# Batched 64x64 matmul: the left operand transposed into its block diagonal by VectorE, and loaded in 8 KB runs

## The chip, the cores and the metric

The kernel runs on one core of one Trainium2 chip. The metric is the time of one execution on the device in microseconds (us), as the median of several runs; a profile of one execution gives the span from its first to its last instruction.

## The reference

Inputs are `a` and `b`, both 1024 x 64 x 64 in fp32, and the output is their product matrix by matrix, in fp32:

```python
def reference(a, b):
    return np.matmul(a, b).astype(np.float32)
```

Each array is 16.78 MB. The kernel multiplies in bf16 and sums in fp32.

## The kernel before, in words

The 1024 products are done in 16 tiles of 64 (`t`). Four matrices are multiplied at a time. TensorE sums over the 128 partitions, so the kernel gives each of four matrices 32 partitions: a partition holds one pair of neighbouring k. The pair is two bf16 values, and the kernel treats it as one 4-byte word wherever it only moves data (`bitcast(fp32)`). The weights of a matmul are a block diagonal `at_bd`: on the 32 partitions of matrix h only the columns of matrix h are filled, with its transposed a, and the rest stays zero from a memset at the start. There are two such buffers (`N_BD`), used in turn. For each group of four matrices `multiply` (L189) issues two halves of the columns (`j`) times the two members of the pair (`u`), 64 matmuls of 128x64 a tile.

How a gets into `at_bd`:

- `load_a` (L73, L77) fetches 128 matrices (an `s`, two tiles) in runs of 4 KB, 128 partitions a DMA. Three quarters of them are cast to bf16 by the load on GpSimd's queue, with `single_packet`; the last quarter comes plain, in fp32, on SP's queue. The first 128 matrices come plain on both SP's and ScalarE's queue (`load_first_a`, L90).
- `regroup` (L105, L108, L111) copies, and where needed casts, them into `a_bf`, on VectorE.
- `transpose` (L120) turns 128x128 words at a time on TensorE, with an identity, into PSUM, 16 for each `s`; ScalarE copies the result to `at_sb` (L123), and reorders it.
- `spread` (L133) copies from `at_sb` into the four diagonal blocks, four VectorE copies of 32x1024 words a tile.

b is loaded a tile at a time (L96, on SP's queue for even `t` and on ScalarE's for odd), three tiles ahead (`B_AHEAD`), and cast to bf16 by VectorE (L144; the first on ScalarE, the last in quarters on both). The products lie in PSUM and are copied to `o_sb` in pieces of 64x512 (L177), mostly by ScalarE, with 14 of them by VectorE. A tile is stored one tile later (`HOLD`), from GpSimd's queue, and the last two tiles from SP's and ScalarE's (L166).

The order on each engine is the order of the calls, written out by hand (`manual_schedule`). In the loop over `t` come `spread(t+1)`, `cast(t+1)`, the load of b three tiles ahead, a load of a, a transpose for the next `s`, `multiply(t)`, and then `regroup`, another transpose and the store of the tile before. An instruction waits at the head of its engine's queue for its inputs and for its buffer; everything behind it on that queue waits with it. `a_pool` holds three `s`, `o_pool` eight tiles.

Of the kernel before, what the change touches and what calls it, by code (L numbers as in the profile page):

```python
# [7 lines left out]

fp32 = mybir.dt.float32
# [4 lines left out]
def kernel(  # L14
# [7 lines left out]

    nc = tc.nc
    B, M, K = a.shape  # L30
    _, _, N = b.shape
    assert (M, K, N) == (64, 64, 64) and B % 128 == 0

    n_t, n_s = B // 64, B // 128
    A_AHEAD = 3
    B_AHEAD = 3
    N_BD = 2
    HOLD = 2

    a_v = a.rearrange("(s g h) (mp v) k -> s h g mp (v k)", h=4, g=32, v=16)  # L40
    b_v = b.rearrange("(t g h) (kp u) n -> t (h kp) g (u n)", h=4, g=16, u=2)
    o_v = out.rearrange("(t gh x) (mo w) n -> t (x mo) gh (w n)", gh=8, x=8, w=4)

    consts = ctx.enter_context(tc.tile_pool(name="consts", bufs=1))
    a_pool = ctx.enter_context(tc.tile_pool(name="a_pool", bufs=A_AHEAD))
    b_pool = ctx.enter_context(tc.tile_pool(name="b_pool", bufs=B_AHEAD))
    work = ctx.enter_context(tc.tile_pool(name="work", bufs=2))
    o_pool = ctx.enter_context(tc.tile_pool(name="o_pool", bufs=8))
    t_psum = ctx.enter_context(
        tc.tile_pool(name="t_psum", bufs=4, space=bass.MemoryType.PSUM)  # L50
    )
    o_psum = ctx.enter_context(
        tc.tile_pool(name="o_psum", bufs=2, space=bass.MemoryType.PSUM)
    )

    bd_tiles = [
        consts.tile([128, 2, 16, 2, 4, 16], fp32, name=f"at_bd{i}") for i in range(N_BD)
    ]
    identity = consts.tile([128, 128], fp32)
    warm = consts.tile([128, 2], fp32)  # L60
    a_tiles, b_tiles, abf_tiles, at_tiles, bbf_tiles = {}, {}, {}, {}, {}
    held = {}

    def store_queue(t, lo):
        if t < n_t - 2:
            return nc.gpsimd
        return nc.scalar if t == n_t - 1 and lo % 4 == 0 else nc.sync

    def load_a(s):

        a_sb = a_pool.tile([128, 3, 16, 64], bf16, name="a_sb")
        for h in range(3):
            nc.gpsimd.dma_start(  # L73
                out=a_sb[:, h, :, :].rearrange("p v k -> p (v k)"), in_=a_v[s, h], single_packet=True
            )
        a_raw = a_pool.tile([128, 16, 64], fp32, name="a_raw")
        nc.sync.dma_start(out=a_raw[:].rearrange("p v k -> p (v k)"), in_=a_v[s, 3])  # L77
        a_tiles[s] = a_sb, a_raw

    def load_first_a():  # L80

        raw = [
            o_pool.tile([128, 8, 2, 2, 64], fp32, name="o_sb")[:].rearrange(
                "p gh j wl n -> p (gh j wl n)"
            )
            for _ in range(2)
        ]
        parts = [raw[h % 2][:, 1024 * (h // 2) : 1024 * (h // 2) + 1024] for h in range(4)]
        for h in range(4):
            (nc.scalar if h % 2 else nc.sync).dma_start(out=parts[h], in_=a_v[0, h])  # L90
        a_tiles[0] = parts

    def load_b(t):
        b_sb = b_pool.tile([128, 16, 128], fp32, name="b_sb")
# [1 line left out]
        queue.dma_start(out=b_sb[:], in_=b_v[t])  # L96
        b_tiles[t] = b_sb

    def regroup(s):
        a_sb = a_tiles.pop(s)  # L100
        a_bf = work.tile([128, 16, 4, 64], bf16, name="a_bf")
        if s == 0:
            for h in range(4):
                copy = nc.scalar.copy if h % 2 else nc.vector.tensor_copy
                copy(a_bf[:, :, h, :], a_sb[h].rearrange("p (v k) -> p v k", v=16))  # L105
        else:
            cast_sb, raw = a_sb
            nc.vector.tensor_copy(  # L108
                a_bf[:, :, 0:3, :], cast_sb[:].rearrange("p h v k -> p v h k")
            )  # L110
            nc.vector.tensor_copy(a_bf[:, :, 3, :], raw[:])  # L111
        abf_tiles[s] = a_bf
        at_tiles[s] = work.tile([128, 2, 32, 2, 4, 4], fp32, name="at_sb")

    def transpose(s, j):
        a_cols = abf_tiles[s][:].rearrange("p v h k -> p v (h k)").bitcast(fp32)
        for wl in range(2):
            at_ps = t_psum.tile([128, 4, 128], fp32, name="at_ps")
            for vo in range(4):
                nc.tensor.transpose(  # L120
                    at_ps[:, vo, :], a_cols[:, 4 * vo + 2 * j + wl, :], identity[:]
                )
            nc.scalar.copy(  # L123
                at_tiles[s][:, j, :, wl, :, :],
                at_ps[:].rearrange("p vo (g mp) -> p g mp vo", mp=4),
            )

    def spread(t):
        half = slice(16 * (t % 2), 16 * (t % 2) + 16)
        bd = bd_tiles[t % N_BD]  # L130
        for h in range(4):
            rows = slice(32 * h, 32 * h + 32)
            nc.vector.tensor_copy(  # L133
                bd[rows, :, :, :, h, :].rearrange("p j g wl mo -> p j (g wl) mo"),
                at_tiles[t // 2][rows, :, half, :, :, :].rearrange(
                    "p j g wl mp vo -> p j (g wl) (mp vo)"
                ),
            )

    def cast(t):  # L140
# [15 lines left out]
            piece()  # L156

    def multiply(t):
        at_bd = bd_tiles[t % N_BD][:].rearrange("p j g wl h mo -> p j g (wl h mo)")
        at_bd = at_bd.bitcast(bf16).rearrange("p j g (c u) -> p j g c u", u=2)  # L160
        b_bf = bbf_tiles.pop(t)
        last = t == n_t - 1
# [6 lines left out]
            )  # L169

        def evacuate(o_ps, gh, n, copies):

            for par in range(2):
                for wl in range(2):
                    src = o_ps[64 * wl : 64 * wl + 64, :, par, :, :]
                    dst = o_sb[64 * par : 64 * par + 64, gh : gh + n, :, wl, :]
                    copies[2 * par + wl](dst, src)  # L177

        for half in range(2):
            if not last:  # L180
                o_ps = o_psum.tile([128, 4, 2, 2, 64], fp32, name="o_ps")
            for g8 in range(8):
                if last and g8 % 4 == 0:
                    o_ps = t_psum.tile([128, 2, 2, 2, 64], fp32, name="at_ps")
                g = 8 * half + g8
                gl = (g8 % 4 if last else g8) // 2
                for j in range(2):
                    for u in range(2):
                        nc.tensor.matmul(  # L189
                            o_ps[:, gl, g % 2, j, :],  # L190
                            at_bd[:, j, g, :, u],
                            b_bf[:, g, 64 * u : 64 * u + 64],
                            start=(u == 0),
                            stop=(u == 1),
                        )
                if last and g8 % 4 == 3:
                    copy = nc.scalar.copy if g8 == 3 else nc.vector.tensor_copy
                    evacuate(o_ps, g // 4 * 2, 2, [copy] * 4)
            if not last:
                copies = [nc.scalar.copy] * 4  # L200
                if half and t % 2:
                    copies[2:] = [nc.vector.tensor_copy] * 2
                evacuate(o_ps, 4 * half, 4, copies)
        if last:
            held[t] = [lambda q=q: put(2 * q, 2) for q in range(4)]
        else:
# [1 line left out]
            held[t] = [lambda q=q: put(q, 8 if whole else 4) for q in ([0] if whole else [0, 4])]  # L208

    with tc.manual_schedule():  # L210
        load_first_a()

        nc.vector.memset(warm[:, 0:1], 0.0)
        nc.scalar.copy(warm[:, 1:2], warm[:, 0:1])  # L214
        load_b(0)
        load_b(1)
        nc.vector.memset(bd_tiles[0][:], 0.0)  # L217
        make_identity(nc, identity)
        nc.gpsimd.memset(bd_tiles[1][:, 0], 0.0)
        load_a(1)  # L220
        load_b(2)
        nc.gpsimd.memset(bd_tiles[1][:, 1], 0.0)
        load_a(2)
        regroup(0)
        transpose(0, 0)
        transpose(0, 1)
        spread(0)
        cast(0)
        for t in range(n_t):
            s, half = t // 2, t % 2  # L230
            if t + 1 < n_t:
                spread(t + 1)
                cast(t + 1)
            if t + B_AHEAD < n_t:
                load_b(t + B_AHEAD)
            if half == 0 and 0 < s < n_s - 1 - A_AHEAD:
                load_a(s + 1 + A_AHEAD)
            if half == 0 and 0 < s < n_s - 1:
                transpose(s + 1, 1)
            multiply(t)  # L240
            if t == 0:
                regroup(1)
                load_a(A_AHEAD)
                load_a(A_AHEAD + 1)
                transpose(1, 0)
                transpose(1, 1)
            elif t == 1:
                regroup(2)
            elif half == 0 and s + 2 < n_s:
                regroup(s + 2)  # L250
            if half == 1 and s + 2 < n_s:
                transpose(s + 2, 0)
            if t >= HOLD - 1:
                store(t - HOLD + 1)
        for t in range(n_t - HOLD + 1, n_t):
            store(t)
# [30 lines left out]
```

## Time and profile before

| What | Value |
| --- | --- |
| median of 3 runs | 134.8 us (134.71 to 134.83) |
| span of the profiled execution | 133.4 us |
| busy: TensorE matmul / weight load | 64.4 / 61.1 us |
| busy: VectorE | 94.6 us (71%), 120 instructions |
| busy: ScalarE | 87.9 us (66%), 161 instructions |
| busy: GpSimd | 33.0 us (25%) |
| packets of the DMA engines | 45.01 MB, mean 337 GB/s |
| mean granted TensorE clock | 0.785 of full speed |

The span lies 1.4 us under the median; it leaves out what is before the first and after the last instruction. A group of the profile names the line and engine, the operation, what is written and read with their shapes (partitions x elements), how often it ran, then busy time in us and the mean of one in ns, and after the bar how long the engine stood idle just before and who ended most of that. In the slices of the span each digit is the busy share of one fortieth, in tenths. Packets of loads that cast are counted by the bytes they write, half of what they read.

### The profile page before, as it was taken

The numbers are of one execution on the slowest core, as the hardware profiler recorded it, in microseconds if no ns is written. First come the engines' busy times: TensorE is split into PE (matmuls) and PEld (weight loads), VectorE is DVE, ScalarE is ACT, GpSimd is POOL, SyncE is SP. The second block draws the span as 40 slices with busy tenths as digits, with TensorE's granted clock in tenths as the row PEclk, the third lists the DMA queues.
The fourth block names the chain that finished last, engine by engine and source line by source line (L and its number), as shares of the span: only waits on it lengthen the run. The fifth ranks groups of instructions, "written<-read, shape, count | busy, mean of one in ns | idle before, by whom it ended". The sixth has DMA issues, their size and how long they took to land.

```text
span 133.4 us, 2837 instructions
## 1 busy us (share of the span) xinstructions
PE 64.4 (48%) x1152; PEld 61.1 (46%) x1152; DVE 94.6 (71%) x120; ACT 87.9 (66%) x161; POOL 33.0 (25%) x43
## 2 busy tenths in 40 slices
PE   0006406960089384289518970956197363970000
PEld 0006306950089274189418950945196363960000
DVE  5930399109998809995999699959999995987000
ACT  3225424999036998969595969696968969099600
POOL 8991000420090070341233021203020410300000
PEclk9999975797557999856985699599959955599555
DMA  3999999999999999999999999999999999999990
GB/s 77 371 329 311 307 311 281 284 306 325 327 312 401 316 320 333 399 384 397 311 281 375 406 389 351 304 316 390 394 396 387 396 392 391 402 405 398 382 319 18
DMA packets 19021, 45.01 MB, mean 337 GB/s; under 512 B 1088, under 2 KB 3136, under 8 KB 19008
## 3 DMA queue, kind: packets, MB, share of 16 engines
q0 software_dynamic: 6832, 20.19, 50.1%
q1 hardware_dynamic: 7120, 14.68, 30.4%
q10 hardware_dynamic: 5056, 9.96, 19.7%
q8 instruction: 9, 0.15, 0.4%
q14 instruction: 4, 0.03, 0.1%
HBM read 33.55 MB, written 16.78 MB: 377 GB/s over the span
## 4 chain that ended last, share of the span: by engine, by line
DMA 53%; DVE 15%; ACT 13%; PE 6%; issue 5%; SPq 2%; DVEq 0%; ACTq 0%
DMA b_sb<-in_b_dram 53%; ACT o_sb L177 9%; DVE at_bd L133 6%; PE o_ps L189 4%; DVE b_bf L144 4%; DVE o_sb L177 3%; PE at_ps L120 2%; ACT at_sb L123 2%; ACT b_bf L144 1%; SPq L90 1%; DVE a_bf L108 1%; SPq L96 1%; ACT b_bf L151 1%; DVE a_bf L111 0%; SPq L77 0%
## 5 line engine op out<-in xcount | busy, mean ns | idle before, releaser
L177 ACT COPY o_sb<-o_ps 64x512 f32<-64x512 f32 x106 | 61.5, 580 | 10.3 <-PE o_ps L189 9.0
L189 PEld LDWEIGHTS <-at_bd 128*128 128x128 bf16 x1024 | 42.3, 113 | 39.5 <-DVE b_bf L144 25.7
L189 PE MATMUL o_ps<-b_bf,at_bd 128*128 128x64 bf16 x960 | 42.6, 216 | 35.4 <-DVE b_bf L144 23.4
L133 DVE COPY at_bd<-at_sb 32x1024 f32<-32x1024 f32 x64 | 46.9, 733 | 14.1 <-ACT at_sb L123 11.8
L120 PE MATMUL at_ps<-identity,a_bf 128*128 128x128 f32 x128 | 21.2, 335 | 19.4 <-ACT a_bf L105 11.2
L166 POOL DMA_DIRECT2D out_dram<-o_sb x14 | 15.4, 1097 | 56.9 <-ACT at_sb L123 23.4
L120 PEld LDWEIGHTS at_ps<-identity,a_bf 128*128 128x128 f32 x128 | 19.3, 180 | 19.5 <-issue 19.5
L123 ACT COPY at_sb<-at_ps 128x512 f32<-128x512 f32 x32 | 17.5, 590 | 11.0 <-PE at_ps L120 7.8
L144 DVE CAST b_bf<-b_sb 128x2048 bf16<-128x2048 f32 x14 | 17.8, 1271 | 9.6 <-DMA b_sb<-in_b_dram 9.4
L73 POOL DMA_DIRECT2D a_sb<-in_a_dram x21 | 13.6, 662 | 26.4 <-DVE a_bf L108 19.4
L177 DVE COPY o_sb<-o_ps 64x512 f32<-64x512 f32 x14 | 9.7, 690 | 0.3
L108 DVE COPY a_bf<-a_sb 128x3072 bf16<-128x3072 bf16 x7 | 6.7, 950 | 0.0
L105 ACT CAST a_bf<-o_sb 128x1024 bf16<-128x1024 f32 x2 | 2.1, 1044 | 5.2 <-DMA o_sb<-in_a_dram 5.2
L111 DVE CAST a_bf<-a_raw 128x1024 bf16<-128x1024 f32 x7 | 4.8, 683 | 0.0
L144 ACT CAST b_bf<-b_sb 128x2048 bf16<-128x2048 f32 x1 | 1.9, 1900 | 3.9 <-DMA b_sb<-in_b_dram 3.9
L105 DVE CAST a_bf<-o_sb 128x1024 bf16<-128x1024 f32 x2 | 2.8, 1382 | 1.9 <-DMA o_sb<-in_a_dram 1.9
L217 DVE MEMSET at_bd<- 128x4096 f32 x1 | 3.5, 3472 | 0.8 <-issue 0.8
L177 DVE COPY o_sb<-at_ps 64x256 f32<-64x256 f32 x8 | 3.4, 422 | 0.5 <-PE at_ps L189 0.4
L151 ACT CAST b_bf<-b_sb 128x512 bf16<-128x512 f32 x2 | 1.1, 615 | 3.6 <-DMA b_sb<-in_b_dram 3.6
L177 ACT COPY o_sb<-at_ps 64x256 f32<-64x256 f32 x8 | 2.9, 366 | 0.1
L214 ACT ACT_TABLE_LOAD x1 | 1.3, 1283 | 2.3 <-issue 2.3
L189 PE MATMUL at_ps<-b_bf,at_bd 128*128 128x64 bf16 x64 | 2.0, 193 | 1.0 <-DVE at_bd L133 1.0
(12 smaller groups left out, 6.1 us busy)
## 6 DMA issues: line engine op xcount, KB each, us to landing
out_dram<-o_sb POOLq DMA_DIRECT2D x14, 1024.0 KB, 21.6
a_sb<-in_a_dram POOLq DMA_DIRECT2D x21, 256.0 KB, 16.4
a_raw<-in_a_dram SPq DMA_DIRECT2D x7, 512.0 KB, 18.7
o_sb<-in_a_dram SPq DMA_DIRECT2D x2, 512.0 KB, 5.9
o_sb<-in_a_dram ACTq DMA_DIRECT2D x2, 512.0 KB, 7.1
out_dram<-o_sb SPq DMA_DIRECT2D x2, 512.0 KB, 7.5
out_dram<-o_sb SPq DMA_DIRECT2D x2, 256.0 KB, 7.8
out_dram<-o_sb ACTq DMA_DIRECT2D x2, 256.0 KB, 5.5
```

The lines of the kernel that those rows point to most:

```text
L73: nc.gpsimd.dma_start(out=a_sb[:, h, :, :].rearrange("p v k -> p (v k)"), in_=a_v[s, h], single_packet=True)
L105: copy(a_bf[:, :, h, :], a_sb[h].rearrange("p (v k) -> p v k", v=16))
L108: nc.vector.tensor_copy(a_bf[:, :, 0:3, :], cast_sb[:].rearrange("p h v k -> p v h k"))
L111: nc.vector.tensor_copy(a_bf[:, :, 3, :], raw[:])
L120: nc.tensor.transpose(at_ps[:, vo, :], a_cols[:, 4 * vo + 2 * j + wl, :], identity[:])
L123: nc.scalar.copy(at_tiles[s][:, j, :, wl, :, :], at_ps[:].rearrange("p vo (g mp) -> p g mp vo", mp=4),)
L133: nc.vector.tensor_copy(bd[rows, :, :, :, h, :].rearrange("p j g wl mo -> p j (g wl) mo"), at_tiles[t // 2][rows, :, half, :, :, :].rearrange(
L144: (nc.vector.tensor_copy if t else nc.scalar.copy)(b_bf[:], b_sb[:])
L166: store_queue(t, lo).dma_start(out=o_v[t, :, lo : lo + n, :], in_=o_sb[:, lo : lo + n].rearrange("p gh j wl n -> p (gh j wl n)"),)
L177: copies[2 * par + wl](dst, src)
L189: nc.tensor.matmul(o_ps[:, gl, g % 2, j, :], at_bd[:, j, g, :, u], b_bf[:, g, 64 * u : 64 * u + 64], start=(u == 0), stop=(u == 1),)
L217: nc.vector.memset(bd_tiles[0][:], 0.0)
```

## The change

a no longer goes through TensorE. A tile's 64 matrices are loaded so that the four matrices of a group lie on different quarters of the partitions: quarter q holds the matrices 4g + q, with 16 x 2 rows, each a run of 8 KB (half a matrix). So a load covers 32 partitions and a tile takes four of them. Tiles 0, 4, 8 and 12 (`RAW`) come plain, on SP's queue (tile 0 also on ScalarE's), and are cast by ScalarE (tile 0 by both VectorE and ScalarE); the other twelve are cast by the load, on GpSimd's queue, without `single_packet`. a is loaded six tiles ahead.

`spread` is now four VectorE transposes of 32x32 blocks, 32 partitions x 1024 words each, which write straight into `at_bd`. The layout of `at_bd` is changed so that the 128 columns of a group and half still lie side by side in the same order (`wl`, matrix, row); the eight `vo` of a row are neighbours, and a transposed block writes one word of each of 16 groups x 2 `mp`: 8 words on for the next `mp`, then 248 on for the next group.

`regroup`, `transpose`, the identity, `a_bf`, `at_sb` and their PSUM buffers are gone. `o_psum` has three buffers instead of two, and the last tile has two of its own. All output copies of tiles 0 to 14 are on ScalarE. The matmuls, the loads of b, and the stores are as before.

```diff
-    a_v = a.rearrange("(s g h) (mp v) k -> s h g mp (v k)", h=4, g=32, v=16)
+    a_v = [
+        [
+            a[64 * t + q : 64 * t + 64 : 4].rearrange("g (mp v) k -> g mp (v k)", mp=2)
+            for q in range(4)
+        ]
+        for t in range(n_t)
+    ]
...
-        consts.tile([128, 2, 16, 2, 4, 16], fp32, name=f"at_bd{i}") for i in range(N_BD)
+        consts.tile([128, 16, 4, 4, 2, 8], fp32, name=f"at_bd{i}") for i in range(N_BD)
...
+    def load_a(t):
+        if t in RAW:
+            raw = raw_pool.tile([128, 32, 64], fp32, name="a_raw")
+            raw_tiles[t] = raw
+        else:
+            a_tiles[t] = a_pool.tile([128, 32, 64], bf16, name="a_sb")
+        for q in range(4):
+            rows = slice(32 * q, 32 * q + 32)
+            if t in RAW:
+                queue = nc.scalar if t == 0 and q % 2 else nc.sync
+                queue.dma_start(
+                    out=raw[rows].rearrange("p v k -> p (v k)"), in_=a_v[t][q]
+                )
+            else:
+                nc.gpsimd.dma_start(
+                    out=a_tiles[t][rows].rearrange("p v k -> p (v k)"),
+                    in_=a_v[t][q],
+                )
+
+    def cast_a(t):
+        a_tiles[t] = a_pool.tile([128, 32, 64], bf16, name="a_sb")
+        raw = raw_tiles.pop(t)
+        if t == 0:
+            nc.vector.tensor_copy(a_tiles[t][:, 0:16, :], raw[:, 0:16, :])
+            nc.scalar.copy(a_tiles[t][:, 16:32, :], raw[:, 16:32, :])
+        else:
+            nc.scalar.copy(a_tiles[t][:], raw[:])
...
     def spread(t):
-        half = slice(16 * (t % 2), 16 * (t % 2) + 16)
         bd = bd_tiles[t % N_BD]
-        for h in range(4):
-            rows = slice(32 * h, 32 * h + 32)
-            nc.vector.tensor_copy(
-                bd[rows, :, :, :, h, :].rearrange("p j g wl mo -> p j (g wl) mo"),
-                at_tiles[t // 2][rows, :, half, :, :, :].rearrange(
-                    "p j g wl mp vo -> p j (g wl) (mp vo)"
-                ),
+        pairs = a_tiles.pop(t)[:].rearrange("p v k -> p (v k)").bitcast(fp32)
+        pairs = pairs.rearrange("p (vo w kp) -> p w vo kp", vo=8, w=4)
+        for q in range(4):
+            rows = slice(32 * q, 32 * q + 32)
+            nc.vector.transpose(
+                bd[rows, :, :, q, :, :].rearrange("p g w mp vo -> p w vo g mp"),
+                pairs[rows],
             )
...
-                copies = [nc.scalar.copy] * 4
-                if half and t % 2:
-                    copies[2:] = [nc.vector.tensor_copy] * 2
-                evacuate(o_ps, 4 * half, 4, copies)
+                evacuate(o_ps, 4 * half, 4, [nc.scalar.copy] * 4)
...
+        load_a(0)
...
+        load_a(1)
         nc.vector.memset(bd_tiles[0][:], 0.0)
...
+        load_a(2)
+        load_a(3)
+        nc.gpsimd.memset(bd_tiles[1][:, 0:8], 0.0)
+        load_a(4)
+        nc.gpsimd.memset(bd_tiles[1][:, 8:16], 0.0)
+        load_a(5)
+        cast_a(0)
         spread(0)
         cast(0)
         for t in range(n_t):
             if t + 1 < n_t:
+                if t + 1 in RAW:
+                    cast_a(t + 1)
                 spread(t + 1)
                 cast(t + 1)
             if t + B_AHEAD < n_t:
                 load_b(t + B_AHEAD)
+            if t + A_AHEAD < n_t:
+                load_a(t + A_AHEAD)
             multiply(t)
             if t >= HOLD - 1:
                 store(t - HOLD + 1)
```

More of the change, by code (lines that the diff above doesn't have):

```diff
@@ L5 @@
 from concourse import bass_utils, mybir
-from concourse.masks import make_identity
 from concourse._compat import with_exitstack
@@ L31 @@
     _, _, N = b.shape
-    assert (M, K, N) == (64, 64, 64) and B % 128 == 0
-    n_t, n_s = B // 64, B // 128
-    A_AHEAD = 3
+    assert (M, K, N) == (64, 64, 64) and B % 64 == 0
+    n_t = B // 64
+    A_AHEAD = 6
     B_AHEAD = 3
@@ L38 @@
     HOLD = 2
-    a_v = a.rearrange("(s g h) (mp v) k -> s h g mp (v k)", h=4, g=32, v=16)
-    b_v = b.rearrange("(t g h) (kp u) n -> t (h kp) g (u n)", h=4, g=16, u=2)
+    RAW = (0, 4, 8, 12)
+    a_v = [
[5 more added lines that the diff above has]
+    ]
+    b_v = b.rearrange("(t g q) (kp u) n -> t (q kp) g (u n)", q=4, g=16, u=2)
     o_v = out.rearrange("(t gh x) (mo w) n -> t (x mo) gh (w n)", gh=8, x=8, w=4)
@@ L45 @@
     a_pool = ctx.enter_context(tc.tile_pool(name="a_pool", bufs=A_AHEAD))
+    raw_pool = ctx.enter_context(tc.tile_pool(name="raw_pool", bufs=2))
     b_pool = ctx.enter_context(tc.tile_pool(name="b_pool", bufs=B_AHEAD))
@@ L48 @@
     o_pool = ctx.enter_context(tc.tile_pool(name="o_pool", bufs=8))
-    t_psum = ctx.enter_context(
-        tc.tile_pool(name="t_psum", bufs=4, space=bass.MemoryType.PSUM)
-    )
-    o_psum = ctx.enter_context(
-        tc.tile_pool(name="o_psum", bufs=2, space=bass.MemoryType.PSUM)
+    o_psum = ctx.enter_context(
+        tc.tile_pool(name="o_psum", bufs=3, space=bass.MemoryType.PSUM)
+    )
+    q_psum = ctx.enter_context(
+        tc.tile_pool(name="q_psum", bufs=2, space=bass.MemoryType.PSUM)
     )
     bd_tiles = [
-        consts.tile([128, 2, 16, 2, 4, 16], fp32, name=f"at_bd{i}") for i in range(N_BD)
+        consts.tile([128, 16, 4, 4, 2, 8], fp32, name=f"at_bd{i}") for i in range(N_BD)
     ]
-    identity = consts.tile([128, 128], fp32)
     warm = consts.tile([128, 2], fp32)
-    a_tiles, b_tiles, abf_tiles, at_tiles, bbf_tiles = {}, {}, {}, {}, {}
-    held = {}
+    a_tiles, raw_tiles, b_tiles, bbf_tiles, held = {}, {}, {}, {}, {}
     def store_queue(t, lo):
@@ L67, in store_queue @@
         return nc.scalar if t == n_t - 1 and lo % 4 == 0 else nc.sync
[L69 to L88, printed above, removed]
-        for h in range(4):
-            (nc.scalar if h % 2 else nc.sync).dma_start(out=parts[h], in_=a_v[0, h])
-        a_tiles[0] = parts
+    def load_a(t):
[24 more added lines that the diff above has]
+            nc.scalar.copy(a_tiles[t][:], raw[:])
     def load_b(t):
@@ L97, in load_b @@
         b_tiles[t] = b_sb
[L99 to L107, printed above, removed]
-            nc.vector.tensor_copy(
[L109 to L126, printed above, removed]
     def spread(t):
-        half = slice(16 * (t % 2), 16 * (t % 2) + 16)
         bd = bd_tiles[t % N_BD]
-        for h in range(4):
-            rows = slice(32 * h, 32 * h + 32)
-            nc.vector.tensor_copy(
-                bd[rows, :, :, :, h, :].rearrange("p j g wl mo -> p j (g wl) mo"),
-                at_tiles[t // 2][rows, :, half, :, :, :].rearrange(
-                    "p j g wl mp vo -> p j (g wl) (mp vo)"
-                ),
+        pairs = a_tiles.pop(t)[:].rearrange("p v k -> p (v k)").bitcast(fp32)
[5 more added lines that the diff above has]
+                pairs[rows],
             )
@@ L158, in multiply @@
     def multiply(t):
-        at_bd = bd_tiles[t % N_BD][:].rearrange("p j g wl h mo -> p j g (wl h mo)")
+        at_bd = bd_tiles[t % N_BD][:].rearrange("p g (j wl) q mp vo -> p j g (wl q mp vo)", j=2)
         at_bd = at_bd.bitcast(bf16).rearrange("p j g (c u) -> p j g c u", u=2)
@@ L183, in multiply @@
                 if last and g8 % 4 == 0:
-                    o_ps = t_psum.tile([128, 2, 2, 2, 64], fp32, name="at_ps")
+                    o_ps = q_psum.tile([128, 2, 2, 2, 64], fp32, name="q_ps")
                 g = 8 * half + g8
@@ L210 @@
     with tc.manual_schedule():
-        load_first_a()
+        load_a(0)
         nc.vector.memset(warm[:, 0:1], 0.0)
@@ L216 @@
         load_b(1)
+        load_a(1)
         nc.vector.memset(bd_tiles[0][:], 0.0)
-        make_identity(nc, identity)
-        nc.gpsimd.memset(bd_tiles[1][:, 0], 0.0)
-        load_a(1)
         load_b(2)
-        nc.gpsimd.memset(bd_tiles[1][:, 1], 0.0)
         load_a(2)
-        regroup(0)
-        transpose(0, 0)
-        transpose(0, 1)
+        load_a(3)
[4 more added lines that the diff above has]
+        cast_a(0)
         spread(0)
@@ L229 @@
         for t in range(n_t):
-            s, half = t // 2, t % 2
             if t + 1 < n_t:
+                if t + 1 in RAW:
+                    cast_a(t + 1)
                 spread(t + 1)
@@ L235 @@
                 load_b(t + B_AHEAD)
[L236 to L239, printed above, removed]
+            if t + A_AHEAD < n_t:
+                load_a(t + A_AHEAD)
             multiply(t)
[L241 to L252, printed above, removed]
             if t >= HOLD - 1:
```

## The prediction, written before the changed kernel ran

> **What bounds the kernel now.** I read the slices of the span first, because they show which resource never rests.
>
> ```profile
> PE   0006406960089384289518970956197363970000
> ...
> DVE  5930399109998809995999699959999995987000
> ACT  3225424999036998969595969696968969099600
> ...
> DMA  3999999999999999999999999999999999999990
> GB/s 77 371 329 311 307 311 281 284 306 325 327 312 401 316 320 333 399 384 397 311 281 375 406 389 351 304 316 390 394 396 387 396 392 391 402 405 398 382 319 18
> ```
>
> One digit is 3.3 us. The DMA engines are at 9 from the second slice to the last but one; every compute engine has gaps. The GB/s row swings from 281 to 406 and settles near 395 in the last quarter, when only b loads and stores are left (the a loads are issued up to 66 us). Loads that cast count only the bytes they write, so the low figures of the first half are no slower transfer. The bytes at HBM say it better:
>
> ```profile
> HBM read 33.55 MB, written 16.78 MB: 377 GB/s over the span
> ```
>
> These are 50.33 MB, and at the 393 GB/s of the stretch from 100 to 128 us they take 128.1 us. With about 2 us before the first packet and 3 us of draining that is the whole span of 133.4 us. Next I read the chain of waits:
>
> ```profile
> DMA 53%; DVE 15%; ACT 13%; PE 6%; issue 5%; SPq 2%; DVEq 0%; ACTq 0%
> ```
>
> Half of the chain is landings of b, and the rest is work that frees buffers for them. So **transfers set the time**, and 16 tiles of 64 matrices come at 133.4/16 = 8.3 us each. A compute engine becomes the bound only when it needs over 8.3 us a tile. VectorE is the nearest, with 94.6 us in all. The measured median, 134.8 us, is 1.4 us above the profiled span; I add 1.4 to each sum.
>
> **Bytes and transfers.** HBM bytes stay the same: a, b and out once each. Before, the first 128 matrices of a come plain, and of each later 128 three quarters are cast by the load; after, 12 of 16 tiles are cast and 4 come plain. What changes is form: 4 KB runs into 128 partitions become 8 KB runs into 32 partitions, four DMAs a tile. No row has either, so I bound it. Best case: all 50.33 MB go at 393 GB/s or somewhat above, and a start about 1 us earlier, because GpSimd now issues loads before its memsets (before, its first a load is issued at 3.0 us): 132 to 134 us. Worst case: loads into a quarter of the partitions move at half the rate. For the 4.19 MB of plain loads that is 4.19/0.393 = 10.7 us more, 145.5 us. I take zero, between a gain of 2 us and a loss of 10.7, because as long as something else sets the pace it is hidden.
>
> [...]
>
> **TensorE and ScalarE.** Gone are 128 transposes (L120, 21.2 us) and 32 copies (L123, 17.5 us). ScalarE gets 14 copies that VectorE did (14 x 0.58 = 8.1 us) and three casts of 128x2048 (the L144 row, 1.90 us each: 5.7). ScalarE's tile is 8 x 0.58 = 4.6 us, or 6.5 with a cast, under 8.3: cost nothing, covered by transfers, and by VectorE if that is slower. TensorE keeps 64 matmuls a tile, 3.3 us in the chain. GpSimd issues 48 a loads instead of 21: at the 0.66 us of L73 that is 32 us, with 15.4 of stores and two memsets of 1.85 still under half the span. A POOL load waits only for the transposes six tiles back, and the store queued behind it has nothing earlier to do. SP issues 14 a loads instead of 9; load 8 waits for the raw buffer of tile 0, long free, so the b loads behind it are not held.
>
> **VectorE, the term that decides.** These are the rows:
>
> ```profile
> L133 DVE COPY at_bd<-at_sb 32x1024 f32<-32x1024 f32 x64 | 46.9, 733 | 14.1 <-ACT at_sb L123 11.8
> L120 PE MATMUL at_ps<-identity,a_bf 128*128 128x128 f32 x128 | 21.2, 335 | 19.4 <-ACT a_bf L105 11.2
> ...
> L144 DVE CAST b_bf<-b_sb 128x2048 bf16<-128x2048 f32 x14 | 17.8, 1271 | 9.6 <-DMA b_sb<-in_b_dram 9.4
> ...
> L177 DVE COPY o_sb<-o_ps 64x512 f32<-64x512 f32 x14 | 9.7, 690 | 0.3
> ...
> L177 DVE COPY o_sb<-at_ps 64x256 f32<-64x256 f32 x8 | 3.4, 422 | 0.5 <-PE at_ps L189 0.4
> ```
>
> Removed: 64 copies (46.9), 14 copies of outputs (9.7), 14 regroupings (6.7 + 4.8), and part of the first group's casts. Added: 64 transposes of 32x1024 words and one cast of 128x1024 (0.68). The whole price is that of one transpose, and no row has one. **Low end:** the two L177 rows give VectorE's slope for single words, (690 - 422)/256 = 1.047 ns an element, and a fixed 154 ns; a transpose at that slope takes 0.154 + 1.024 x 1.047 = 1.23 us. **High end:** the only row that transposes these same words is TensorE's L120, 335/128 = 2.62 ns a column; VectorE at that rate takes 2.84 us. What lies between is the write. Every VectorE row of before writes runs of 16 words or more. The transpose writes each word 32 B, then 992 B, from the last one. I take twice the slope, 2.09 ns, as if each word paid once to go in and once to be put down alone: **2.30 us**. That is nearer to the only row that transposes than to the copies.
>
> [...]
>
> **The sum.** The first tile needs 1.05 MB of a. Before, the first two 512 KB pieces are in at 6.3 us (the first ScalarE cast starts at 6.34); with half of the cast on each engine (0.68 and 1.04 us), the first transpose starts at about 8 us. From there VectorE has work in hand without a pause: spread(t+1) waits for multiply(t-1), 3.3 us of TensorE that end while spread(t) and its cast still run; loads are six tiles (a) and three tiles (b) ahead. So:
> - start: 8.0
> - 64 transposes of 2.30 and 0.02 of issue: 148.5
> - 14 casts of b of 1.27: 17.8
> - two quarter casts of the last b, 0.42 each: 0.85
> - end: in before the last VectorE copy ends 3.9 us after the last cast; then an issue and a 256 KB store (5.5 us to land), 9 in all, a little less than the rows as the queues are no longer full.
> That is 184.2 us, and with 1.4 around it **186 us** (+38%). A tile then takes 4 x 2.32 + 1.27 = 10.6 us against 8.3 of transfers: the engine has become the bound. With the price p of a transpose left open, the time is 38.3 + 64 p, and it meets 134.8 at p = 1.50 us. Below that transfers hide it.
>
> **Rivals.**
> - **Transposes at the copy slope (p = 1.23 us): not slower.** VectorE needs 6.2 us a tile, under 8.3; 38.3 + 64 x 1.23 = 117 us is less than the transfers, which stay the bound. The time is that of the transfers, 132 to 134 us (133 in the middle: the best case above), with nothing else in the way. For it: VectorE rows follow element counts closely. Against: no row writes words apart. It decides up to p = 1.50 us.
> - **Transfers to 32 partitions are slower, and VectorE hides nothing of it (p below 1.5).** 135 to 146 us, with 145.5 when the plain loads run at half rate. For it: four DMAs of 256 KB in place of one of 512 KB, each to a quarter of the partitions. Against: before mixes three queues, and the engines have stores to do beside.
> - **Forecast, VectorE bound:** p from 1.6 to 2.84 gives 141 to 220 us.
>
> **Chances.** VectorE bound 0.76; transfers bound and quicker 0.13, and within 0.2% of before 0.03 (0.2% is about what a measurement of this kernel can tell from no change); transfers slower 0.08. Faster 0.13, same 0.03, slower 0.76 + 0.08 = 0.84. The range for 8 in 10 leaves out the faster case (0.13) and the top of the first, p above 2.65 (0.07): 134 to 208 us. The likeliest case has 186.
>
> **What would show each step.** The transpose row: 2.30 us mean, DVE busy near 170 us and at 9 in all slices from the third. DMA digits below 9 in the middle, with HBM near 273 GB/s over the span; the chain mostly DVE at_bd. If DMA stays at 9 throughout and the transpose row shows 1.2 us, the forecast is wrong in that one term. If DMA is at 9 and its GB/s are lower in stretches of plain loads, the second rival holds. A gap on VectorE behind multiply or a load would break the sum too.

## The result, and the profile after

The changed kernel takes 166.64 us (median, 165.77 to 167.85) against 134.81 us before: a ratio of 1.235, with a 95% interval of 1.229 to 1.241. The forecast was 186 us (134 to 208). The profiled execution took 166.69 us, with a span of 164.9 us. Some runs of a kernel are a per cent or two slower than its others, so ratios and intervals compare the quicker runs alone, while medians are over all runs.

From the page of the changed kernel, the slices of the span (one digit is now 4.1 us):

```profile
PE   0000007706234170807052341608080624426350
...
DVE  6259996899989999999999999999999999999761
ACT  3020015992948264462949082745947190947460
...
DMA  4999999999999999999999999999896785107724
GB/s 117 224 235 239 244 245 241 241 242 252 390 396 307 228 311 351 275 385 293 390 328 361 311 358 324 337 342 398 302 308 213 252 258 203 56 8 246 254 97 162
```

VectorE is at 8 or 9 from the fourth slice nearly to the end, but for the seventh (6), where it had many gaps before. But the DMA engines are at 8 or 9 as well, up to 124 us, and in the first 40 us they move only some 240 GB/s. Both rows are full at once for about two thirds of the span, so the slices alone don't say which of the two sets the time. The groups and the total of the bytes, from the same page:

```profile
HBM read 33.55 MB, written 16.78 MB: 305 GB/s over the span
...
DMA 46%; DVE 24%; issue 15%; POOL 8%; PE 2%; ACT 2%; DVEq 0%; POOLq 0%
...
L110 DVE STREAM_TRANSPOSE at_bd<-a_sb 32x1024 f32<-32x1024 f32 x64 | 123.6, 1931 | 3.8 <-PE o_ps L163 2.0
L151 ACT COPY o_sb<-o_ps 64x512 f32<-64x512 f32 x120 | 69.5, 579 | 38.6 <-PE o_ps L163 23.0
...
L119 DVE CAST b_bf<-b_sb 128x2048 bf16<-128x2048 f32 x14 | 17.2, 1232 | 0.8 <-DMA b_sb<-in_b_dram 0.4
```

A transpose takes 1.93 us, between the two ends of the prediction (1.23 and 2.84) and below the value taken (2.30). What VectorE waited for, from its waits, is little:

```profile
DVE a_sb L93 <- DMA a_raw<-in_a_dram: 4.7, 1, 4.7
DVE o_sb L151 <- PE q_ps L163: 2.3, 2, 1.2
DVE at_bd L110 <- PE o_ps L163: 2.0, 1, 2.0
...
DVE b_bf L119 <- DMA b_sb<-in_b_dram: 0.4, 1, 0.4
```

Columns are the total in us, how often, and the longest. The first is the wait for tile 0 and the second belongs to the tail. Between the start of its first transpose (10.95 us) and the end of its last cast (155.8 us) VectorE stands only 4.4 us of 144.8. The chain of waits, followed back from the end, nevertheless gives transfers 46%. From the end to 108 us it runs along VectorE, and before that along loads of a and stores, so two things were late together there, and the profile alone doesn't settle which.

### The profile page after: what moved, and what is told of

The parts are those of the page before. It is cut to its first block, busy times and chain, and to the rows that moved or that the text cites. A ratio compares the mean times of both kernels' runs of the same rounds, so it can differ in the third digit from the quotient of the medians.

```text
span 164.9 us, 2590 instructions
## 1 busy us (share of the span) xinstructions
PE 56.0 (34%) x1024; PEld 53.7 (33%) x1024; DVE 148.1 (90%) x91; ACT 83.9 (51%) x145; POOL 45.4 (28%) x68
## 4 chain that ended last, share of the span: by engine, by line
DMA 46%; DVE 24%; issue 15%; POOL 8%; PE 2%; ACT 2%; DVEq 0%; POOLq 0%
DMA out_dram<-o_sb 24%; DMA a_sb<-in_a_dram 22%; DVE at_bd L110 22%; POOL a_sb L84 4%; ACT o_sb L151 2%; POOL out_dram L141 1%; DVE b_bf L119 1%; PE q_ps L163 1%; PE o_ps L163 1%; POOL at_bd L192 1%; POOL at_bd L194 1%; DVE o_sb L151 1%; DVEq L239 0%; DVEq L110 0%; POOLq L84 0%
## 5 line engine op out<-in xcount | busy, mean ns | idle before, releaser
L110 DVE STREAM_TRANSPOSE at_bd<-a_sb 32x1024 f32<-32x1024 f32 x64 | 123.6, 1931 | 3.8 <-PE o_ps L163 2.0
L151 ACT COPY o_sb<-o_ps 64x512 f32<-64x512 f32 x120 | 69.5, 579 | 38.6 <-PE o_ps L163 23.0
L163 PEld LDWEIGHTS <-at_bd 128*128 128x128 bf16 x1024 | 53.7, 129 | 106.0 <-DVE b_bf L119 74.7
L163 PE MATMUL o_ps<-b_bf,at_bd 128*128 128x64 bf16 x960 | 52.1, 238 | 98.8 <-DVE b_bf L119 72.8
L84 POOL DMA_DIRECT2D a_sb<-in_a_dram x48 | 28.2, 599 | 39.8 <-DMA out_dram<-o_sb 22.9
L119 DVE CAST b_bf<-b_sb 128x2048 bf16<-128x2048 f32 x14 | 17.2, 1232 | 0.8 <-DMA b_sb<-in_b_dram 0.4
L101 ACT MOVE_SHAPE b_sb<-in_b_dram x8 | 0.5, 64 | 12.9 <-DVE b_bf L119 12.9
L96 ACT CAST a_sb<-a_raw 128x2048 bf16<-128x2048 f32 x3 | 5.7, 1899 | 0.1
L163 PE MATMUL q_ps<-b_bf,at_bd 128*128 128x64 bf16 x64 | 3.9, 241 | 5.0 <-DVE at_bd L110 4.2
L151 DVE COPY o_sb<-q_ps 64x256 f32<-64x256 f32 x8 | 3.4, 422 | 2.4 <-PE q_ps L163 2.3
L151 ACT COPY o_sb<-q_ps 64x256 f32<-64x256 f32 x8 | 2.9, 366 | 3.4 <-issue 2.2
L192 POOL MEMSET at_bd<- 128x2048 f32 x1 | 1.8, 1823 | 0.0
L194 POOL MEMSET at_bd<- 128x2048 f32 x1 | 1.8, 1823 | 0.0
```

The costliest lines, as they stand in the source:

```text
L84: nc.gpsimd.dma_start(out=a_tiles[t][rows].rearrange("p v k -> p (v k)"), in_=a_v[t][q],)
L96: nc.scalar.copy(a_tiles[t][:], raw[:])
L110: nc.vector.transpose(bd[rows, :, :, q, :, :].rearrange("p g w mp vo -> p w vo g mp"), pairs[rows],)
L119: (nc.vector.tensor_copy if t else nc.scalar.copy)(b_bf[:], b_sb[:])
L163: nc.tensor.matmul(o_ps[:, gl, g % 2, j, :], at_bd[:, j, g, :, u], b_bf[:, g, 64 * u : 64 * u + 64], start=(u == 0), stop=(u == 1),)
L192: nc.gpsimd.memset(bd_tiles[1][:, 0:8], 0.0)
```

## The experiments

The theory at this point, W: a transpose costs 1.93 us because it writes single words that aren't neighbours, and VectorE, full with that, sets the time. Rivals: O, the transpose of 4-byte words is slow whatever it writes; and P, the loads into 32 partitions have become slow and VectorE only follows them. The first experiment adds N: what runs beside the transpose slows it.

### One transpose, by itself

A kernel with one load, then four calls each of seven VectorE operations on 32x1024 words, nothing beside them; the products are left out.

```diff
+    p_rec = pool.tile([128, 16, 4, 4, 2, 8], fp32, name="as_after")
+    p_pair = pool.tile([128, 16, 4, 4, 8, 2], fp32, name="pairs")
+    p_run = pool.tile([128, 4, 4, 8, 32], fp32, name="runs")
+    p_far = pool.tile([128, 32, 4, 4, 8], fp32, name="far")
...
             nc.vector.transpose(
+                p_rec[rows, :, :, q, :, :].rearrange("p g w mp vo -> p w vo g mp"), src[rows]
             )
...
+            nc.vector.transpose(
+                p_pair[rows, :, :, q, :, :].rearrange("p g w vo mp -> p w vo g mp"), src[rows]
             )
...
+            nc.vector.transpose(p_run[rows, :, q, :, :], src[rows])
...
+            nc.vector.transpose(
+                p_far[rows, :, :, q, :].rearrange("p c w vo -> p w vo c"), src[rows]
+            )
```

In `as_after` a word is written 8 or 248 words on from the last one, in `pairs` two words are neighbours, in `runs` 32 are, and in `far` there are 128 words from one to the next. Three plain copies (`tensor_copy`) write as the first three transposes do.

> VectorE alone, after one load, nothing beside it; the products are left out (the output holds only the buffers written). Four calls each, 32x1024 words, of: a transpose that writes as the changed kernel does (steps of 8 and 248 words), one whose words come in pairs, one whose 32 words lie side by side, one with 128 words between words, and three plain copies with the first three of these write patterns. Theory W (the writing of lone words costs the time): 1.9 us as in the changed kernel, then 1.25 us for pairs and 1.23 for runs, about 1.9 or more for the far steps; the copy slows down with lone words too, from 0.69 us to over 1 us. Theory O (the transpose of 4-byte words itself is slow): all four transposes 1.9 us, the three copies 0.69 us. Theory N (neighbours on the chip slow it): all transposes about 1.23 us here.

Its groups:

```profile
L44 DVE STREAM_TRANSPOSE as_after<-src 32x1024 f32<-32x1024 f32 x4 | 7.6, 1889 | 0.1
L57 DVE STREAM_TRANSPOSE far<-src 32x1024 f32<-32x1024 f32 x4 | 7.6, 1888 | 0.1
L49 DVE STREAM_TRANSPOSE pairs<-src 32x1024 f32<-32x1024 f32 x4 | 4.9, 1237 | 0.1
L54 DVE STREAM_TRANSPOSE runs<-src 32x1024 f32<-32x1024 f32 x4 | 4.9, 1236 | 0.1
...
L62 DVE COPY c_after<-src 32x1024 f32<-32x1024 f32 x4 | 4.5, 1123 | 0.1
...
L68 DVE COPY c_pairs<-src 32x1024 f32<-32x1024 f32 x4 | 2.9, 720 | 0.1
L74 DVE COPY c_runs<-src 32x1024 f32<-32x1024 f32 x4 | 2.7, 685 | 0.1
```

W holds. The only difference between the first and the third row is which words are neighbours, and it is 0.65 us of 1.89. Two neighbouring words were enough (1.237 us), a run of 32 brought nothing more (1.236), and between the two distances of lone words tried (8 and 248, or 128) there was no difference (1.889 and 1.888). A copy pays too: 1.12 us against 0.69. O falls, as the pairs are quick, and so does N, as the lone words are slow with nothing beside them; in the kernel they take another 0.04 us. Less the fixed 154 ns of the prediction, a lone word costs 1.69 ns and a word of a pair 1.06, close to the slope that the prediction had from two rows (1.047).

### The kernel with pairs

```diff
-        consts.tile([128, 16, 4, 4, 2, 8], fp32, name=f"at_bd{i}") for i in range(N_BD)
+        consts.tile([128, 16, 4, 4, 8, 2], fp32, name=f"at_bd{i}") for i in range(N_BD)
...
-                bd[rows, :, :, q, :, :].rearrange("p g w mp vo -> p w vo g mp"),
+                bd[rows, :, :, q, :, :].rearrange("p g w vo mp -> p w vo g mp"),
...
-        at_bd = bd_tiles[t % N_BD][:].rearrange("p g (j wl) q mp vo -> p j g (wl q mp vo)", j=2)
+        at_bd = bd_tiles[t % N_BD][:].rearrange("p g (j wl) q vo mp -> p j g (wl q vo mp)", j=2)
```

`multiply` takes the columns in the order in which they now lie, so the rows of each product come out in another order; the work is the same.

> The changed kernel with the last two dimensions of the block diagonal swapped, so that the transposes write pairs of neighbouring words; the rows of each product come out in another order, all else is the same work. Theory W: transposes 1.25 us, VectorE 6.3 us a tile, so transfers set the time: 134 us if the new form of the loads costs nothing, up to 146 if it does. Theory O: transposes 1.93 us and 166 us.

It took 147.49 us, ratio 1.095 (1.089 to 1.102). From its page:

```profile
DVE  5429792094790968779069399999985999999530
...
DMA  4999999999999999999999999999999999999874
...
HBM read 33.55 MB, written 16.78 MB: 343 GB/s over the span
...
DMA 68%; issue 12%; DVE 10%; POOL 4%; ACT 2%; PE 2%; DVEq 0%; POOLq 0%
...
L110 DVE STREAM_TRANSPOSE at_bd<-a_sb 32x1024 f32<-32x1024 f32 x64 | 79.1, 1236 | 11.0 <-ACT a_sb L96 4.5
```

And from its waits:

```profile
DVE b_bf L119 <- DMA b_sb<-in_b_dram: 18.5, 7, 5.0
```

The transposes take 1.24 us, VectorE has gaps again, the DMA engines are at 9 to the end, and VectorE's waits for loads of b rise from 0.4 to 18.5 us. So with VectorE out of the way the transfers set the time, and they are 12.7 us slower than before. The 44.5 us taken from VectorE gave 19.

### VectorE given more, and less

More: each cast of b done twice, 14 x 1.25 us.

```diff
+            if t:
+                nc.vector.tensor_copy(b_bf[:], b_sb[:])
```

> The changed kernel with each of VectorE's 14 casts of b done twice. If VectorE sets the time of the changed kernel: 166.6 + 14 x 1.25 = 184 us. If the loads do and VectorE only follows: 167 to 172 us.

182.16 us, ratio 1.350 (1.345 to 1.356): 15.5 of the 17.5 us arrive. In its profile the 2.0 us that VectorE waited behind the first multiply are gone, which accounts for the rest. That is a bound that adds up, and speaks for VectorE and against P.

Less: those casts on ScalarE. First in their place, which is ahead of the output copies; then behind the output copies, with the casts of plain tiles.

```diff
-            (nc.vector.tensor_copy if t else nc.scalar.copy)(b_bf[:], b_sb[:])
+            nc.scalar.copy(b_bf[:], b_sb[:])
```

> The changed kernel with all casts of b on ScalarE instead of VectorE (14 of 1.23 us less on VectorE; ScalarE 6.5 us a tile, 8.4 with a cast of a). If VectorE is the bound: 166.6 - 17.2 = 149 us, with VectorE still busy in nearly every slice. If the start or the loads set the pace instead: 163 us or more.

```diff
             multiply(t)
+            if t + 2 < n_t:
+                if t + 2 in RAW:
+                    cast_a(t + 2)
+                cast(t + 2)
```

> The changed kernel with all casts of b on ScalarE, as in e3_casts_on_scalar, but each cast (of b, and of a where it is plain) behind the output copies of the tile two before, so that nothing waits behind a cast for a load. If e3 gained nothing because the casts stood ahead of the output copies in ScalarE's queue and waited there for b: 166.6 - 17.2 = 149 us, near the 147.5 of the kernel with pairs, where the transfers set the time. If VectorE is not what bounds the changed kernel: 163 us or more again.

166.38 us (ratio 1.232, 1.224 to 1.239) and 167.15 us (1.239, 1.235 to 1.244): nothing gained, in both. Taken by the words of the expectations, VectorE would not be the bound. The second kernel's transposes and two of its waits show where the gain went:

```profile
L110 DVE STREAM_TRANSPOSE at_bd<-a_sb 32x1024 f32<-32x1024 f32 x64 | 123.3, 1927 | 19.2 <-ACT a_sb L96 14.1
```

```profile
ACT b_bf L119 <- DMA b_sb<-in_b_dram: 30.2, 7, 12.9
DVE at_bd L110 <- ACT a_sb L96: 14.1, 3, 9.6
```

17.2 us of work left VectorE, and its idle time before transposes rose from 3.8 us to 19.2. 14.1 of them are for ScalarE's casts of the three plain tiles. On ScalarE these stand behind a cast of b that waits for its load. The casts of b(3) and of the plain tile 4 in this kernel, and that of tile 4 in the changed one, each with its start and length in us:

```profile
45.62 1.90 ACT L119 CAST b_bf<-b_sb 128x2048 bf16<-128x2048 f32 x1 [4.66 <-DMA b_sb<-in_b_dram]
...
52.31 1.90 ACT L96 CAST a_sb<-a_raw 128x2048 bf16<-128x2048 f32 x1
```

```profile
45.36 1.90 ACT L96 CAST a_sb<-a_raw 128x2048 bf16<-128x2048 f32 x1
```

So the transposes of tile 4 start at 54.2 us; in the changed kernel, where ScalarE has no cast of b to wait at, they start at 48.0, after VectorE's other work. From there the shorter tile (7.8 us for 9.0) saves some 13 us. The later start (6.3), two more waits for casts of plain tiles (4.5) and the last casts of b, which now stand between transposes (0.8), take nearly all of it back: the last transposes end at 153.4 us for 155.0.

So these two kernels made a new wait in place of the work that they took away, and neither shows what VectorE's relief is worth by itself; the kernel with pairs does. They do show how near the loads are: in the changed kernel too VectorE waits 0.4 us for b(3), at 46.8 us. A version with the casts on ScalarE that avoids the wait was not tried.

### The loads

Loads of a alone, in seven stretches of 4.19 MB read, one after the other; nothing is computed.

```diff
+        hw = [nc.sync, nc.scalar]
...
+        def quarters_near(dst):
+            for t in range(4):
+                quarters(dst, hw, t, (0, 1, 2, 3))
...
+            (0, whole_8k),
+            (0, whole_4k),
+            (0, quarters_near),
+            (0, quarters_far),
+            (1, cast_4k),
+            (1, cast_quarters_near),
+            (1, cast_quarters_far),
```

> Loads of a alone, 4.19 MB read in each of seven stretches, one after the other, nothing computed (the products are left out). Plain on SP's and ScalarE's queues: 128 partitions in runs of 8 KB; 128 partitions in runs of 4 KB; 32 partitions in runs of 8 KB, the two queues on neighbouring quarters (0 and 1, then 2 and 3); the same with the queues on quarters 0 and 2, then 1 and 3. Cast, on GpSimd's queue: 128 partitions in runs of 4 KB; 32 partitions in runs of 8 KB, quarters in order; and in the order 0, 2, 1, 3. Theory P (few partitions make a load slow): the first two stretches about 10.5 us (400 GB/s), the neighbouring quarters near 20 us, quarters 0 and 2 together between; the casts in quarters slower than the cast into 128 partitions. Theory S (a load is slow because it is small or its runs are long): all four kinds of quarters alike, and 8 KB differs from 4 KB into 128 partitions.

A window inside each stretch, in that order; the last two columns are the DMA engines' share and GB/s, which count a cast by what it writes:

```profile
3.00:12.00 9.00, 0.00 (x0) 0.00 (x0) 1.00 1.00 421
16.00:26.00 10.00, 0.00 (x0) 0.00 (x0) 1.00 1.00 398
30.00:48.00 18.00, 0.00 (x0) 0.00 (x0) 1.00 1.00 214
52.00:68.00 16.00, 0.00 (x0) 0.00 (x0) 1.00 0.99 245
72.00:81.00 9.00, 0.00 (x0) 2.30 (x5) 1.00 1.10 201
86.00:96.00 10.00, 0.00 (x0) 5.17 (x11) 1.00 1.03 180
100.00:111.00 11.00, 0.00 (x0) 5.68 (x12) 1.00 0.98 177
```

Plain loads into 32 partitions, on two queues at once, moved together at half the rate, 214 GB/s against 421, with the DMA engines just as "busy" (1.00). For whole stretches VectorE's waits for their loads tell it, first 4 KB runs into 128 partitions, then quarters:

```profile
27.12 0.18 DVE L98 COPY plain<-plain 128x8 f32<-128x8 f32 x1 [13.42 <-DMA plain<-in_a_dram]
49.41 0.17 DVE L98 COPY plain<-plain 128x8 f32<-128x8 f32 x1 [22.11 <-DMA plain<-in_a_dram]
```

That is 22.1 us against 13.4, so 2.2 us more for a tile of 1.05 MB. Two queues on quarters 0 and 2 helped little (245 for 214). Casts into 32 partitions wrote 180 GB/s for 201: 14.0 us against 12.9, 0.28 us a tile; they also differ in run length (8 KB for 4 KB) and go without `single_packet`. Into 128 partitions, runs of 8 KB in loads of 1.05 MB (12.8 us) gained 0.6 us on runs of 4 KB in loads of half that (13.4). The plain quarters are smaller loads too, 262 KB each, and no stretch has loads of that size into 128 partitions. The casts in quarters read just as little in each load and lost a tenth of their rate, not half; how much of the loss of the plain ones is due to size is not shown.

In the kernel with pairs, then: the quarters in another order, and fewer plain tiles.

```diff
-        for q in range(4):
+        for q in (0, 2, 1, 3):
...
-                queue = nc.scalar if t == 0 and q % 2 else nc.sync
+                queue = nc.scalar if t == 0 and q >= 2 else nc.sync
```

> The kernel with pairs (rows of the products in another order), with the quarters of a loaded in the order 0, 2, 1, 3 on each queue, and for tile 0 quarters 0 and 1 on SP and 2 and 3 on ScalarE. If what costs is that neighbouring quarters collide and others don't: 136 to 142 us instead of 147.5. If each small load is slow by itself: 147.5 within 1.

```diff
-    RAW = (0, 4, 8, 12)
+    RAW = (0,)
```

> The kernel with pairs, with only tile 0 loaded plain and tiles 4, 8 and 12 cast by the load like the others (ScalarE has three casts less). If the plain loads into 32 partitions are what costs, three quarters of the loss go: 138 us. If the loads that cast cost as much for each byte read, 147.5 us, within 1; if they cost more, slower.

The order gives 146.37 us, ratio 1.084 (1.078 to 1.090) for 1.095 (1.089 to 1.102) without it: at the edge of what these runs can tell, and far from the 136 to 142 us of colliding neighbours. One plain tile instead of four gives 141.01 us, ratio 1.037 (1.034 to 1.039) for 1.095. That is 7.9 us less by the ratios and 6.5 by the medians; three tiles at 2.2 us alone would be 6.5. VectorE's waits for loads of b fall from 18.5 us to 6.3, so the transfers did get quicker. But the edit also takes three casts off ScalarE, for which VectorE waited 4.5 us in the kernel with pairs, and the two are not separated. So the plain tiles, their loads above all, are most of what the new form of the loads costs, and the remaining 5 us are near what tile 0 (2.2) and fifteen cast tiles (4.2) would cost by the stretches alone, a sum that is only argued.

In the changed kernel the same edit tells whether this is hidden:

> The changed kernel with only tile 0 loaded plain. In the kernel with pairs this took 6.5 us off. If the slow loads are hidden behind VectorE in the changed kernel: 166.6, within 2 (VectorE's sum is the same; a little less if its wait at the start goes). If both add up: 160 us.

165.54 us, ratio 1.226 (1.222 to 1.231) for 1.235 (1.229 to 1.241): 1.1 us less. So what costs up to 7.9 us in the kernel with pairs is hidden behind VectorE here, and P falls.

Last, the same form in the kernel before: its loads of a split into four of 32 partitions, all of them, the plain ones, and those that cast.

```diff
-            nc.gpsimd.dma_start(
-                out=a_sb[:, h, :, :].rearrange("p v k -> p (v k)"), in_=a_v[s, h], single_packet=True
-            )
+            for r in range(0, 128, 32):
+                nc.gpsimd.dma_start(
+                    out=a_sb[r : r + 32, h, :, :].rearrange("p v k -> p (v k)"),
+                    in_=a_v[s, h, r // 4 : r // 4 + 8],
+                    single_packet=True,
+                )
...
-        nc.sync.dma_start(out=a_raw[:].rearrange("p v k -> p (v k)"), in_=a_v[s, 3])
+        for r in range(0, 128, 32):
+            nc.sync.dma_start(
+                out=a_raw[r : r + 32].rearrange("p v k -> p (v k)"),
+                in_=a_v[s, 3, r // 4 : r // 4 + 8],
+            )
```

> The kernel before, with each load of a after the first 128 matrices split into four of 32 partitions; runs of 4 KB, queues and bytes as they are. If a load into 32 partitions moves as fast as one into 128: 134.8 us, within 1. If it moves at half the rate where it is plain and alone: 135 to 145 us, with GB/s below 300 in the first half.

> The kernel before with only the plain loads of a after the first 128 matrices (7 of 524 KB) split into four of 32 partitions. By the stretches measured alone (22.1 us against 13.4 for 4.19 MB) 3.67 MB cost 3.67/4.19 x 8.7 = 7.6 us: 142.4 us. If stores beside them hide it: 135 to 138 us.

> The kernel before with only the loads that cast (21 of 524 KB read) split into four of 32 partitions. By the stretches measured alone (14.0 us against 12.9 for 4.19 MB) 11.0 MB cost 2.9 us: 137.7 us. If it is the number of loads in flight on GpSimd's queue that costs, as its waits of 24.8 us for its own loads in b1_loads_in_quarters suggest: 145 us or more, and DMA digits of 5 to 8.

All: 154.77 us, ratio 1.145 (1.136 to 1.154). Plain alone: 151.22 us, ratio 1.120 (1.117 to 1.124), 16 us more and twice the 7.6 of the stretches alone. Casts alone: 149.54 us (146.85 to 149.89, without an interval), 12 to 15 us more, four to five times the 2.9. All three miss their forecasts from the rate alone, and the two parts add up to more than the whole. These loads read 128 KB each, half as much as those of the changed kernel, and there are four where one was. The page of the kernel with all of them shows DMA gaps, and its waits show GpSimd waiting for loads of its own queue to land:

```profile
DMA  3999999977999999988999989999799999999992
```

```profile
POOL a_sb L74 <- DMA a_sb<-in_a_dram: 24.8, 30, 2.8
```

With the casts alone the time is that forecast for too many loads in flight on GpSimd's queue (145 us or more), but the DMA digits of 5 to 8 that were to come with it don't: all but one between the ends are 9. So in this kernel splitting costs by more than the rate into 32 partitions. What part is the number of loads, their size, or the collision with other queues' loads stays open; it wasn't taken further, as it isn't in the changed kernel's time.

## Why the prediction was right, and where it was not

The direction, the cause and the range were right; the size was 186 for 166.6. Its sum against the profiled execution:

| Step | Forecast, us | Measured, us |
| --- | --- | --- |
| first transpose starts | 8.0 | 10.95 |
| 64 transposes | 147.2 | 123.6 |
| issue between instructions (measured: gaps less overlaps) | 1.3 | 0.8 |
| 14 casts of b | 17.8 | 17.2 |
| two quarter casts | 0.85 | 0.85 |
| waits of VectorE | 0 | 2.4 |
| from the last cast to the end | 9 | 9.1 |
| span | 184.2 | 164.9 |

- **The transpose: the mechanism right, the size off.** The bounds 1.23 and 2.84 us held. The 2.30 between them, "twice the slope, as if each word paid once to go in and once to be put down alone", was mis-sized, and no row stood behind it: lone words cost 1.6 times the slope (1.69 ns for 1.06), not twice. That alone is 23.6 us; the later start and the waits put 5.4 of them back, which leaves most of the 19.3 us by which the span was missed. In the kernel 1.931 us is 1.735 ns a word; by itself the transpose took 1.69, with steps of 8 and 248 words as with steps of 128.
- **VectorE is the bound: right.** Adding work adds time (182.2), and it hardly waits. But the signs named for it came out half: DMA digits stayed at 8 or 9 up to 124 us, HBM moved 305 GB/s and not 273, and the chain gave VectorE 24%. The prediction saw VectorE 2.3 us a tile above the transfers; they were nearer, as VectorE was faster and the transfers slower: relieved, in the kernel with pairs, it gave 19 us, 1.2 a tile.
- **The form of the loads at zero: right for this kernel but for the start, for the reason given (hidden), as the 1.1 us of the version with one plain tile shows.** But the bound was too low. The prediction put the loss at 10.7 us at the most; the kernel with pairs lies 12.7 above before. The plain loads by themselves did move at half the rate (214 GB/s against 421), as its worst case took with no row behind it; it left out the casts (180 for 201). Four loads of 256 KB also came in place of two of 512, not of one as it says.
- **GpSimd's loads: the waits wrong, without harm here.** They were to wait only for the transposes six tiles back. In the changed kernel those are 1.3 us of their waits; for stores to land they waited 22.9 us, and for loads of their own queue to land 14.1. As VectorE hardly waits, this was hidden.
- **The first rival was priced wrong.** With the transpose at 1.24 us it was to take 132 to 134 us; that kernel took 147.5. The second rival, slower transfers, would have come true in its place, a little beyond its 146. The two rivals were put as if they excluded one another; but p below 1.5 us only says that transfers set the time, and whether that is 133 or 146 us is then the second rival's question.
- **The start: 3 us late.** Four loads into 32 partitions took longer than two into 128 for the same 1.05 MB; tile 0's casts start at 9.9 us for 6.3 in before. GpSimd's loads also start earlier beside them (1.3 us for 3.0), and what part is theirs is not shown. From 5 to 30 us before and after moved, by the profile of each:

```profile
DMA packets 3578, 7.81 MB, mean 312 GB/s; under 512 B 238, under 2 KB 238, under 8 KB 3577
```

```profile
DMA packets 2484, 5.99 MB, mean 240 GB/s; under 512 B 387, under 2 KB 387, under 8 KB 2424
```

The first is before, the second after, and loads that cast count by what they write. The first tile's b came only at 24.0 us, and with it the 2.0 us that VectorE waited behind the first multiply.

## What to carry to other kernels

Before a transpose or copy writes "straight into place", look at the innermost step of what it writes: in the transposes of this kernel lone 4-byte words cost VectorE 1.7 ns each where pairs cost 1.06, and the pair is all it took (1.237 us a transpose for 1.236 in runs of 32). A load's bytes and run length alone don't give its time: split into loads of 32 partitions, plain loads moved at half the rate here (214 GB/s against 421, both in runs of 8 KB). A DMA share of 1.00 went with 214 GB/s as with 421, so read GB/s beside it. And when one engine is found to be the bound, take it out by an experiment before its relief is counted: here 44.5 us off VectorE were worth 19, and 17.2 us moved to ScalarE were worth nothing.

## What the runs showed of the hardware that was not expected

- Alone, casts into 32 partitions lost a tenth of their rate (180 for 201 GB/s written, with runs of 8 KB for 4 KB), plain loads half (214 for 421, both in runs of 8 KB). Why the two differ is not shown.
- Splitting the plain loads of the kernel before into quarters cost 16 us for 3.67 MB, where the rate of the stretches alone gives 7.6.
- In the changed kernel GpSimd's first eight loads go out in 4.1 us, and the ninth waits 1.8 us for one to land. GpSimd waits so 15 times, 14.1 us in all. What sets how many go out before one waits is not shown.
